# A transformer layer's opening on one core: second-half rows squared sooner, one power for four tiles' norms, high parts of values, keys and queries ahead of low ones

## The chip, the cores and the metric

One core of a Trainium2 chip. Its engines run side by side, each with its own instruction stream: PE (TensorE: matrix products and transposes), DVE (VectorE), ACT (ScalarE), POOL (GpSimd) and SP (SyncE, which here issues nearly all DMAs). The metric is the device time of one execution in microseconds (us); lower is better.

## The reference, cut to what matters

```python
h  = rms_norm(x, norm_mix)                     # x: 1024 tokens x 1024 features, float32
P  = h @ w_in                                  # -> q_A k_A v_A | q_B k_B v_B | gate_A gate_B
A  = neighbourhood_attention(rms_norm(q_A), rms_norm(k_A), v_A, rpb)       # 8 heads of 64 ("na")
Bm = sliding_window_attention(rms_norm(q_B), rms_norm(k_B), v_B, sink, t5) # 8 heads, 2 key heads ("sw")
y  = sigmoid(gate_A) * (A @ w_branch_A) + sigmoid(gate_B) * (Bm @ w_branch_B)
x  = x + y @ w_out
x  = x + (silu(rms_norm(x) @ w_gate) * (rms_norm(x) @ w_up)) @ w_down
```

`rms_norm(z) = z / sqrt(mean(z*z) + 1e-6) * gain`. For queries and keys the mean goes over the 64 elements of a head.

## The kernel before

Every float32 product is made of three matmuls of rounded parts: a high part of an operand (rounded by ACT as it copies) and a low part (what is left, by DVE), high x high, high x low and low x high. Tokens lie in 8 tiles of 128; features in 8 blocks of 128 (index k).

The heads come in six groups (`order`): na heads 0 and 1, then sw heads 0 to 3, and so on. This case is about the opening, which is the projection of group 0 (`projection(0)`) and the first tiles of group 1. PE follows the code's order throughout. In the opening (the `opening` stack) ACT, DVE, POOL and SP do too; after it a scheduler orders these four.

In group 0 the eight token tiles go through two passes, c=0 (tiles 0 to 3) and c=1 (tiles 4 to 7), each tile with a PSUM bank of its own; a pass takes k = 0 to 7, and for each k four chunks, one for a tile. A **chunk** is three matmuls of 384 columns (query, key and value columns of the group) in `multiply`. Group 1 and later go tile by tile, eight chunks each, and PE mixes their chunks with the attention of the heads that are ready.

RMSNorm of x is not applied to x. `row_norm(c)` squares four tiles of x on ACT (`rows`, loaded by `load_rows`), with the sums in `rows_rs` and, after a power of -0.5 on POOL, the tokens' factors there; `rows_eps` is the sum's term that belongs inside the head norms. The gates need the same factors spread along columns: `wide_norm(c, ps)` builds four diagonal matrices on DVE (`diag`), multiplies them by ones on PE, and copies the bank to `wide_rs[c]` on ACT.

`finish(tiles)` takes the finished banks of some tiles: ACT squares queries and keys into `qn`, DVE sums them by head into `ss`, POOL adds `rows_eps` and takes the power -0.5, ACT and DVE write high and low values `v`, and DVE multiplies the bank by the norm into `qn`. Then `layout` gives PE work for later: `keys()` transposes the keys of four tiles into a bank `tk`, `pair()` the queries into `tq`, and ACT writes the high half of each head's key or query times the gain, DVE the low half; SP copies keys to `k2`. `pop(pending)` runs the next of these. The names in the trace: `pj` a chunk's bank, `tk` and `tq`, `wg_kh` and `wg_kl` the high and low weights of block k (`after.split(k)` makes those of group 1 during pass c=1), `wst` and `wg_us` their staging tiles.

Softmax of a head's block: `scores` puts q times k into one of two banks `s`, DVE reads the bank with the bias table `bna` into `E`, ACT takes the exponential. `bias_table` adds the table on DVE just ahead of the first block.

Of the kernel before, what the change touches and what calls it, by code (L numbers as in the profile page):

```python
# [19 lines left out]
HD = 64  # L20
NEG = -1e30
EPS = 1e-6
# [3 lines left out]
def block_kernel(ctx, tc, x, xt, small, w_in, rpb, t5, w_ba, w_bb, w_out, w_gate, w_up, w_down,  # L26
# [76 lines left out]
    mhalf = cst.tile([P, 8], F32, name="mhalf")  # L103
# [7 lines left out]

    def rsqrt_mean(dst, ss, n, width):
        nc.gpsimd.tensor_scalar(dst, ss, 1.0 / n, EPS, op0=ALU.mult, op1=ALU.add)
        nc.gpsimd.tensor_tensor(dst, dst, mhalf[:, :width], ALU.pow)
# [27 lines left out]
    def row_norm(c):  # L142
# [5 lines left out]
        nc.gpsimd.tensor_scalar(rows_eps[:, d], rows_rs[:, d], EPS, 1.0, op0=ALU.mult, op1=ALU.mult)  # L148
        nc.gpsimd.tensor_tensor(rows_rs[:, d], rows_rs[:, d], mhalf[:, 0:4], ALU.pow)

    def wide_norm(c, ps):

        dg = slot_u(f"diag{c}")[:, :512]
# [6 lines left out]
    def load_small():  # L160
        nc.scalar.dma_start(cols, small)
        nc.vector.tensor_scalar_mul(nsink, nsink, -1.0)
        for b in "ab":
            nc.vector.tensor_scalar_mul(gq[b], gq[b], HD ** -0.5)
# [65 lines left out]
    def projection(gi, weights, pending, after=None):  # L230
# [14 lines left out]

        def layout(s0):
            sw = kind == "sw"

            def rev_put(z, own, oth, src, g):
# [9 lines left out]
                nc.scalar.activation(to(z, own), src, AF.Copy, scale=g)  # L259
                nc.vector.scalar_tensor_tensor(to(z, oth), src, g, f(to(z, own)), op0=ALU.mult, op1=ALU.subtract)  # L260
# [12 lines left out]
            def put_both(z, own, oth, src, g):  # L273
                nc.scalar.activation(put(z, own), rows16(src), AF.Copy, scale=g)
                nc.vector.scalar_tensor_tensor(put(z, oth), rows16(src), g, f(put(z, own)),
                                               op0=ALU.mult, op1=ALU.subtract)

            def pair(p_):
                tq = bank("pj", f"tq{gi}_{s0}_{p_}")
                for j in range(4):  # L280
                    nc.tensor.transpose(spot(tq, slice(0, P), j), qns[s0 + j][:, tok(p_)], ident)
                for e in range(2):
                    own, oth = slice(e * HD, e * HD + HD), slice(HD - e * HD, 2 * HD - e * HD)
                    rev_put(q[2 * p_ + e], own, oth, tq[own, :], gq[b][own, :])

            def keys():
# [3 lines left out]
                for e in range(nk):  # L290
                    own, oth = slice(e * HD, e * HD + HD), slice(HD - e * HD, 2 * HD - e * HD)
                    put_both(k1[e], own, oth, tk[own, :], gk[b][own, :])
# [19 lines left out]
        def finish(tiles):  # L312

            norms = {}
            for t, ps in tiles:
                ss = norms[t] = ap.tile([P, 8], F32, tag="ss", name=f"ss{gi}_{t}", bufs=4)
                qn = ap.tile([P, 320], F32, tag="qn", name=f"qn{gi}_{t}", bufs=5)
                nc.scalar.activation(qn[:, :nqk], ps[:, :nqk], AF.Square)
                nc.vector.tensor_reduce(ss[:, :nh], qn[:, :nqk].rearrange("p (h e) -> p h e", e=HD),
                                        axis=AX.X, op=ALU.add)  # L320
                nc.gpsimd.tensor_scalar(ss[:, :nh], ss[:, :nh], 1.0 / HD, rows_eps[:, t:t + 1],
                                        op0=ALU.mult, op1=ALU.add)
                nc.gpsimd.tensor_tensor(ss[:, :nh], ss[:, :nh], mhalf[:, :nh], ALU.pow)  # L323
                qns.append(qn)
            for t, ps in tiles:
                rs = rows_rs[:, t:t + 1]
                if kind == "na":
                    for j in range(nk):
                        src = ps[:, nqk + j * HD:nqk + j * HD + HD]
                        nc.scalar.activation(v[j][:, t, 0, :], src, AF.Copy, scale=rs)  # L330
                        nc.vector.scalar_tensor_tensor(v[j][:, t, 1, :], src, rs, f(v[j][:, t, 0, :]),
                                                       op0=ALU.mult, op1=ALU.subtract)
                else:
# [4 lines left out]
                    if t == 7:  # L338
                        vr = slot_v(f"vr{gi}")[:, :512].rearrange("p (b e) -> p b e", e=HD)
                        nc.sync.dma_start(vr, vnat[idx * T:(idx + 1) * T, :].rearrange("(b p) e -> p b e", p=P))  # L340
                        late_v.append(vr)
                nc.vector.tensor_mul(qns[t][:, :nqk].rearrange("p (h e) -> p h e", e=HD),
                                     ps[:, :nqk].rearrange("p (h e) -> p h e", e=HD),
                                     norms[t][:, :nh].unsqueeze(2).to_broadcast([P, nh, HD]))
# [963 lines left out]
```

## Time and profile before

| | |
|---|---|
| time, median of 3 runs | 1357.77 us (1357.66 to 1359.6) |
| profiled execution | 1355.7 us, of which the span of instructions is 1353.8 |
| PE busy in the span | 97% |
| DVE, ACT, POOL busy | 75%, 50%, 13% |

The span runs from the first to the last instruction; what lies around it (1.9 us) is start and end. PE is the engine to watch: a time in which it waits is a time that the kernel could lose, and there is little of it. Start times in the rows below count from the span's start.

### The profile page before, as it was taken

The numbers are of one execution on the slowest core, as the hardware profiler recorded it, in microseconds if no ns is written. First come the engines' busy times: TensorE is split into PE (matmuls) and PEld (weight loads), VectorE is DVE, ScalarE is ACT, GpSimd is POOL, SyncE is SP. The second block draws the span as 40 slices with busy tenths as digits, with TensorE's granted clock in tenths as the row PEclk, the third lists the DMA queues.
The fourth block names the chain that finished last, engine by engine and source line by source line (L and its number), as shares of the span: only waits on it lengthen the run. The fifth ranks groups of instructions, "written<-read, shape, count | busy, mean of one in ns | idle before, by whom it ended". The sixth has DMA issues, their size and how long they took to land.

```text
span 1353.8 us, 19149 instructions
## 1 busy us (share of the span) xinstructions
PE 1318.6 (97%) x6464; PEld 1134.0 (84%) x6464; DVE 1008.8 (75%) x1989; ACT 675.3 (50%) x1381; POOL 174.6 (13%) x320
## 2 busy tenths in 40 slices
PE   9899999999999999999997999999999999999998
PEld 8799999999887887887886888888888888888887
DVE  5578877887769746878978876766777678798775
ACT  6567866785654324535545433333333346263532
POOL 1345544464220000000000000000000000000000
PEclk9899999999999999999998999999999999999999
DMA  8413223132424335747783433223333246672542
GB/s 284 141 50 83 72 69 96 44 104 67 127 86 164 121 97 179 246 159 223 240 280 103 150 102 99 92 90 117 117 117 109 94 130 236 237 259 71 163 133 86
DMA packets 177571, 184.03 MB, mean 136 GB/s; under 512 B 20496, under 2 KB 125968, under 8 KB 177472
## 3 DMA queue, kind: packets, MB, share of 16 engines
q1 hardware_dynamic: 177216, 182.70, 42.6%
q8 instruction: 51, 0.84, 0.3%
q14 instruction: 48, 0.39, 0.1%
q10 hardware_dynamic: 256, 0.10, 0.0%
HBM read 128.74 MB, written 48.97 MB: 131 GB/s over the span
## 4 chain that ended last, share of the span: by engine, by line
PE 80%; DVE 8%; DMA 6%; ACT 3%; issue 1%; POOL 1%; SPq 1%; DVEq 0%; ACTq 0%; POOLq 0%
PE bankZ L771 5%; PE bankZ L772 5%; PE bankZ L773 5%; PE bankY L773 5%; PE bankY L771 5%; PE bankY L772 5%; PE bankX L773 5%; PE bankX L772 5%; PE bankX L771 5%; PE pj L308 3%; PE pj L309 3%; PE pj L310 3%; PE o L587 3%; PE bankV L772 3%; PE bankV L773 2%; PE bankV L771 2%
## 5 line engine op out<-in xcount | busy, mean ns | idle before, releaser
L537 ACT ACTIVATE E<-E,nm 128x384 f32<-128x384 f32 (+3 forms) x128 | 75.7, 592 | 55.1 <-DVE nm L531 47.3
L539 POOL TENSOR_SCALAR E<-E,nm 128x384 f32<-128x384 f32 (+1 forms) x128 | 76.3, 597 | 118.3 <-DVE nm L538 88.5
L51 DVE TENSOR_TENSOR pl<-tp,ph 128x384 fp32r<-128x384 f32 (+1 forms) x128 | 66.5, 520 | 13.1 <-ACT ph L50 11.6
L50 ACT CAST ph<-tp 128x384 fp32r<-128x384 f32 (+1 forms) x128 | 57.4, 448 | 18.4 <-PE tp L549 17.1
L51 DVE TENSOR_TENSOR f<-f 128x512 fp32r<-128x512 f32 x89 | 58.6, 690 | 10.3 <-ACT f L50 10.2
L50 ACT CAST f<-f 128x512 fp32r<-128x512 f32 x89 | 52.7, 619 | 27.1 <-DMA f<-u_dram 26.6
L549 PE MATMUL tp<-ident,E 128*128 128x128 f32 x352 | 59.7, 273 | 0.0
L323 POOL TENSOR_TENSOR ss<-ss,mhalf 128x4 f32<-128x4 f32 (+1 forms) x48 | 51.8, 1079 | 3.4
L587 PE MATMUL o<-pl,v 128*128 128x256 f32 (+2 forms) x160 | 49.3, 308 | 2.4 <-DVE pl L51 2.3
L549 PEld LDWEIGHTS tp<-ident,E 128*128 128x128 f32 x352 | 45.3, 140 | 5.3 <-POOL E L539 0.4
L587 PE MATMUL o<-ph,v 128*128 128x256 f32 (+2 forms) x160 | 46.3, 303 | 2.4 <-DVE of L570 2.3
L525 PE MATMUL s<-k,q 128*128 128x384 f32 (+1 forms) x128 | 46.6, 364 | 0.0
L1140 POOL TENSOR_TENSOR rs<-rs,mhalf 128x4 f32<-128x4 f32 x2 | 2.1, 1059 | 339.9 <-DVE rs L1139 339.9
L1154 ACT ACTIVATE sg<-sg 128x512 f32<-128x512 f32 x44 | 27.9, 633 | 35.4 <-DVE sg L1153 35.2
L526 PE MATMUL s<-k,q 128*128 128x384 f32 (+1 forms) x128 | 41.5, 324 | 0.0
L531 DVE CUSTOM_DVE_ANT_0 E<-s,bsw,cols 128x384 f32<-128x384 f32 (+1 forms) x64 | 37.0, 578 | 5.3 <-PE s L526 4.1
L773 PE MATMUL bankV<-f,f_5l 128*128 128x512 f32 x88 | 35.1, 399 | 3.8 <-DVE f_5l L51 3.8
L531 DVE CUSTOM_DVE_ANT_0 E<-s,bna 128x384 f32<-128x384 f32 (+1 forms) x64 | 33.2, 519 | 6.4 <-PE s L526 5.9
L538 DVE RECIPROCAL nm<-nm 128x1 f32<-128x1 f32 x128 | 20.4, 160 | 23.0 <-ACT E L537 21.6
L773 PE MATMUL bankY<-f,f_6l 128*128 128x512 f32 x88 | 35.1, 399 | 2.2 <-DVE f_6l L51 2.2
L771 PE MATMUL bankV<-f,f_5h 128*128 128x512 f32 x88 | 34.9, 397 | 2.4 <-ACT f_5h L50 2.4
L51 DVE TENSOR_TENSOR f_2l<-wg_s,f_2h 128x512 fp32r<-128x512 f32 x22 | 15.1, 691 | 27.6 <-ACT f_2h L50 27.6
(799 smaller groups left out, 4556.7 us busy)
## 6 DMA issues: line engine op xcount, KB each, us to landing
f<-u_dram SPq DMA_DIRECT2D x77, 256.0 KB
wg_s<-in_w_gate_dram SPq DMA_DIRECT2D x22, 512.0 KB
u_dram<-uT SPq DMA_DIRECT2D x33, 256.0 KB
sg<-g_dram SPq DMA_DIRECT2D x32, 256.0 KB
g_dram<-go SPq DMA_DIRECT2D x24, 256.0 KB
u_dram<-tau SPq DMA_DIRECT2D x22, 256.0 KB
u_dram<-tbu SPq DMA_DIRECT2D x22, 256.0 KB
f<-f_dram SPq DMA_DIRECT2D x18, 256.0 KB
```

The lines of the kernel that those rows point to most:

```text
L50: a = nc.scalar.copy(hi, src)
L51: b = (eng or nc.vector).tensor_tensor(lo, src, f(hi), ALU.subtract)
L323: nc.gpsimd.tensor_tensor(ss[:, :nh], ss[:, :nh], mhalf[:, :nh], ALU.pow)
L525: nc.tensor.matmul(s[:, :n], qs, k1[hd["kl"]][:, ks], start=True, stop=False)
L531: nc.vector.tensor_tensor_reduce(E[:, :n], s[:, :n], hd["bias"](qb), -1.0, sk if sw else 1e30, ALU.add, ALU.min, nm[:, 0:1])
L537: nc.scalar.activation(E[:, :m], E[:, :m], AF.Exp, bias=nm[:, 0:1], scale=-1.0, accum_out=nm[:, 1:2])
L539: nc.gpsimd.tensor_scalar(E[:, :n], E[:, :n], nm[:, 1:2], 1.0, op0=ALU.mult, op1=ALU.mult)
L549: nc.tensor.transpose(tp[:, tok(j)], hd["E"][qq][:, ko:ko + P], ident)
L587: nc.tensor.matmul(hd["O"][half][:, (a - half * 4) * P:(z + 1 - half * 4) * P], v[:, kb].rearrange("p a e -> p (a e)"), pp[:, (a - q0) * P ...
L771: nc.tensor.matmul(ps, hi[:, tok(j)], bh, start=first, stop=False, skip_group_check=True)
L772: nc.tensor.matmul(ps, hi[:, tok(j)], bl, start=False, stop=False, skip_group_check=True)
L773: nc.tensor.matmul(ps, lo[:, tok(j)], bh, start=False, stop=end, skip_group_check=True)
```

## The change

Seven edits, all but one in the opening.

1. The rows of tiles 4 to 7 are loaded behind the second piece of group 1's weights, not after all features of x; the third and fourth pieces and the tables follow them on SP.
2. `row_norm(1)` is issued after block k=4 of pass c=1, not after the pass: ACT has the squares between the high keys and the high queries of the first half.
3. `finish` of four tiles makes one sum and one power of 16 columns on POOL, not four of each with 4 columns. The division by 64 is gone: it sits in `HD * EPS` and in a key gain of 8 rather than a query gain of 1/8.
4. In `finish` all high values, then all low values, then the products with the norm; before, each tile had its own high, low, high, low, product. This holds for later na groups too, two heads at a time.
5. For group 0 both high key parts go ahead of both low ones, and the same for queries (`both`).
6. Transposes of the first half's keys and queries are popped at k=4 and 5 of pass c=1, not 6 and 7. Group 1's weight blocks 0 to 2 are split at k=4, block 3 at k=6, and 4 to 7 at the end. The second half's queries use a bank `t`.
7. `wide_norm` moves from tiles 2 and 3 of group 1 to the first gate's projection, and its diagonals lie in a slot of the weight pool. `qn` has 7 buffers, not 5.

```diff
+        dg = wp.tile([P, 512], F32, tag="whi", name=f"diag{c}", bufs=NWU)
...
+        def both(parts):
+            if gi:
+                for part in parts:
+                    part()()
+            else:
+                for low in [part() for part in parts]:
+                    low()
...
-                ss = norms[t] = ap.tile([P, 8], F32, tag="ss", name=f"ss{gi}_{t}", bufs=4)
...
-                nc.gpsimd.tensor_scalar(ss[:, :nh], ss[:, :nh], 1.0 / HD, rows_eps[:, t:t + 1],
-                                        op0=ALU.mult, op1=ALU.add)
-                nc.gpsimd.tensor_tensor(ss[:, :nh], ss[:, :nh], mhalf[:, :nh], ALU.pow)
...
+            if n == 1:
+                nc.gpsimd.tensor_scalar(ss, ss, 1.0, rows_eps[:, t0:t0 + 1], op0=ALU.mult, op1=ALU.add)
+            else:
+                nc.gpsimd.tensor_tensor(norms, norms, rows_eps[:, t0:t0 + n].unsqueeze(2).to_broadcast([P, n, nh]),
+                                        ALU.add)
+            nc.gpsimd.tensor_tensor(ss, ss, mhalf[:, :n * nh], ALU.pow)
...
+            for t, ps in tiles if kind == "na" else ():
+                for j in range(nk):
+                    nc.vector.scalar_tensor_tensor(v[j][:, t, 1, :], ps[:, nqk + j * HD:nqk + j * HD + HD],
...
-                    if c and k >= 4:
-                        after.split(k - 4)
-                    if c and k >= 6:
+                    for u in {4: (0, 1, 2), 6: (3,)}.get(k, ()) if c else ():
+                        after.split(u)
+                    if c and k in (4, 5):
                         pop(pending)
+                    if c and k == 4:
+                        row_norm(1)
...
-            row_norm(1)
...
-                if gi == 1 and t in (2, 3) and k == 7:
-                    wide_norm(t - 2, bank("pj", f"wide{t}"))
...
+                if i == 0 and not half and k in (1, 4):
+                    wide_norm(k // 4, bank("pj", f"wide{k}"))
...
-        for u in range(4):
+        for u in range(2):
+            weights[1].load(u)
+        for t in range(4, 8):
+            load_rows(t)
+        for u in range(2, 4):
             weights[1].load(u)
...
-        for t in range(4, 8):
-            load_rows(t)
```

ACT's order around the first half's keys and queries (`k_0`, `k_1`, `q_0`, `q_1` are the two heads' operands; `rows_286` and its like are tiles 4 to 7 of x). Before:

```order
L274 ACTIVATE k_0_302<-tk_0_561,cols 64x512
L274 ACTIVATE k_1_303<-tk_0_561,cols 64x512
L50 CAST wg_3h<-wg_1s 128x384
L259 ACTIVATE q_0_298<-tq_0_0_590,cols 64x512
L259 ACTIVATE q_1_299<-tq_0_0_590,cols 64x512
L50 CAST wg_4h<-wst_130 128x384
L50 CAST wg_5h<-wst_130 128x384
L50 CAST wg_6h<-wst_131 128x384
L50 CAST wg_7h<-wst_131 128x384
L146 ACTIVATE rows_286,rows_rs<-rows_286 128x1024
```

Of the change, the same place on ACT:

```order
L282 ACTIVATE k_0_302<-tk_0_528,cols 64x512
L282 ACTIVATE k_1_303<-tk_0_528,cols 64x512
L142 ACTIVATE rows_256,rows_rs<-rows_256 128x1024
L142 ACTIVATE rows_258,rows_rs<-rows_258 128x1024
L142 ACTIVATE rows_260,rows_rs<-rows_260 128x1024
L142 ACTIVATE rows_262,rows_rs<-rows_262 128x1024
L267 ACTIVATE q_0_298<-tq_0_0_560,cols 64x512
L267 ACTIVATE q_1_299<-tq_0_0_560,cols 64x512
L50 CAST wg_3h<-wg_1s 128x384
L50 CAST wg_4h<-wst_130 128x384
```

The four squares of x have moved from behind the weight blocks to a place ahead of the queries, and block 3 of the weights from ahead of the queries to behind them.

POOL's order for the second half (`ss_4` to `ss_7` are head sums of tiles 4 to 7). Before:

```order
L149 TENSOR_TENSOR rows_rs<-rows_rs,mhalf 128x4
L321 TENSOR_SCALAR ss_4_622<-ss_4_622,rows_eps 128x4
L323 TENSOR_TENSOR ss_4_622<-ss_4_622,mhalf 128x4
L321 TENSOR_SCALAR ss_5_628<-ss_5_628,rows_eps 128x4
L323 TENSOR_TENSOR ss_5_628<-ss_5_628,mhalf 128x4
L321 TENSOR_SCALAR ss_6_634<-ss_6_634,rows_eps 128x4
L323 TENSOR_TENSOR ss_6_634<-ss_6_634,mhalf 128x4
L321 TENSOR_SCALAR ss_7_640<-ss_7_640,rows_eps 128x4
L323 TENSOR_TENSOR ss_7_640<-ss_7_640,mhalf 128x4
```

Of the change, POOL from the first half's power on:

```order
L335 TENSOR_TENSOR ss_0_457<-ss_0_457,mhalf 128x16
L143 TENSOR_SCALAR rows_rs<-rows_rs 128x4
L144 TENSOR_SCALAR rows_eps<-rows_rs 128x4
L145 TENSOR_TENSOR rows_rs<-rows_rs,mhalf 128x4
L333 TENSOR_TENSOR ss_4_613<-ss_4_613,rows_eps 128x16
L335 TENSOR_TENSOR ss_4_613<-ss_4_613,mhalf 128x16
L331 TENSOR_SCALAR ss_0_680<-ss_0_680,rows_eps 128x5
```

Eight instructions of 4 columns have become two of 16.

DVE's order ahead of the first softmax (`E_0_0` is the first block's scores out of their bank; `ss_1` to `ss_3` belong to tiles of group 1). Before:

```order
L342 TENSOR_TENSOR qn_1_734<-pj_1_708,ss_1_733 128x320
L275 SCALAR_TENSOR_TENSOR k_0_302<-tk_4_750,cols,k_0_302 64x512
L319 TENSOR_REDUCE ss_2_813<-qn_2_814 128x5
L275 SCALAR_TENSOR_TENSOR k_1_303<-tk_4_750,cols,k_1_303 64x512
L260 SCALAR_TENSOR_TENSOR q_0_298<-tq_4_0_772,cols,q_0_298 64x512
L342 TENSOR_TENSOR qn_2_814<-pj_2_743,ss_2_813 128x320
L260 SCALAR_TENSOR_TENSOR q_1_299<-tq_4_0_772,cols,q_1_299 64x512
L503 TENSOR_TENSOR bna_294<-brna_295,bna_294 128x384 x2
L531 ISA E_0_0_787,nm_0_0_788<-s_0_0_784,bna_294 128x256
```

Of the change:

```order
L327 TENSOR_REDUCE ss_2_784<-qn_2_785 128x5
L356 TENSOR_TENSOR qn_1_716<-pj_1_690,ss_1_715 128x320
L283 SCALAR_TENSOR_TENSOR k_0_302<-tk_4_732,cols,k_0_302 64x512
L283 SCALAR_TENSOR_TENSOR k_1_303<-tk_4_732,cols,k_1_303 64x512
L268 SCALAR_TENSOR_TENSOR q_0_298<-tq_4_0_754,cols,q_0_298 64x512
L268 SCALAR_TENSOR_TENSOR q_1_299<-tq_4_0_754,cols,q_1_299 64x512
L518 TENSOR_TENSOR bna_294<-brna_295,bna_294 128x384 x2
L356 TENSOR_TENSOR qn_2_785<-pj_2_725,ss_2_784 128x320
L327 TENSOR_REDUCE ss_3_832<-qn_3_833 128x5
L546 ISA E_0_0_769,nm_0_0_770<-s_0_0_766,bna_294 128x256
```

The sum `ss_2` now stands ahead of the low keys and queries of the second half, and the sum `ss_3` ahead of the first softmax block.

## Rows read from the trace of the kernel before

**Rows 1.** Windows: span, busy time of PE, PEld, DVE, ACT, POOL; granted clock, DMA.

```profile
60.00:70.00 10.00, 7.50 (x33) 6.93 (x33) 4.62 (x9) 3.79 (x9) 4.12 (x7) 0.73 0.15 33
80.00:345.00 265.00, 261.76 (x1683) 252.98 (x1682) 216.29 (x630) 192.35 (x508) 136.35 (x254) 1.00 0.26 72
```

**Rows 2.** Timeline of PE, pass c=1 ending, group 1 begun: start, length, instruction.

```profile
43.05 0.60 PE L281 MATMUL tq<-ident,qn 128*128 128x128 f32 x4
43.41 0.42 PE L308 MATMUL pj<-wg_0h,h 128*128 128x384 f32 x1
...
45.43 0.34 PE L310 MATMUL pj<-wg_3h,h 128*128 128x384 f32 x1
46.81 0.44 PE L308 MATMUL pj<-wg_4h,h 128*128 128x384 f32 x1 [1.04 <-ACT wg_4h L50]
...
48.11 0.34 PE L308 MATMUL pj<-wg_5h,h 128*128 128x384 f32 x1
```

**Rows 3.** Waits of PE from 42 to 80: sum, times, longest.

```profile
PE tk L289 <- DVE qn L342: 4.6, 4, 1.2
```

**Rows 4.** Timeline of PE around the second half's keys.

```profile
54.36 0.33 PE L308 MATMUL pj<-wg_1h,h 128*128 128x384 f32 x1
...
60.75 0.67 PE L308 MATMUL pj<-wg_2h,h 128*128 128x384 f32 x1
...
65.79 0.33 PE L308 MATMUL pj<-wg_6h,h 128*128 128x384 f32 x1
```

**Rows 5.** Timeline of PE around the two wide norms.

```profile
66.66 0.34 PE L310 MATMUL pj<-wg_7h,h 128*128 128x384 f32 x1
...
70.06 0.44 PE L308 MATMUL pj<-wg_0h,h 128*128 128x384 f32 x1 [1.51 <-ACT wide_rs L158]
...
74.68 1.05 PE L157 MATMUL wide<-diag,ones 128*128 128x128 f32 x8
75.49 0.42 PE L308 MATMUL pj<-wg_0h,h 128*128 128x384 f32 x1
...
76.63 0.34 PE L525 MATMUL s<-k,q 128*128 128x384 f32 x1
```

**Rows 6.** Timeline of ACT, the same stretch.

```profile
45.54 0.68 ACT L259 ACTIVATE q<-tq,cols 64x512 fp32r<-64x512 f32 x1 [0.94 <-DVE q L260]
...
47.90 1.06 ACT L146 ACTIVATE rows<-rows 128x1024 f32<-128x1024 f32 x1
...
52.20 1.21 ACT L318 ACTIVATE qn<-pj 128x256 f32<-128x256 f32 x4
```

**Rows 7.** Timeline of DVE, the same stretch.

```profile
46.25 0.76 DVE L260 SCALAR_TENSOR_TENSOR q<-tq,cols,q 64x512 fp32r<-64x512 f32 x1 [0.75 <-ACT q L259]
47.04 0.56 DVE L51 TENSOR_TENSOR wg_4l<-wst,wg_4h 128x384 fp32r<-128x384 f32 x1
...
52.62 1.40 DVE L319 TENSOR_REDUCE ss<-qn 128x4 f32<-128x256 f32 x4 [2.66 <-ACT qn L318]
...
58.62 0.42 DVE L342 TENSOR_TENSOR qn<-pj,ss 128x256 f32<-128x256 f32 x1 [0.17 <-POOL ss L323]
...
70.43 0.49 DVE L342 TENSOR_TENSOR qn<-pj,ss 128x320 f32<-128x320 f32 x1
...
71.94 1.03 DVE L503 TENSOR_TENSOR bna<-brna,bna 128x384 f32<-128x384 f32 x2
73.00 0.42 DVE L531 CUSTOM_DVE_ANT_0 E<-s,bna 128x256 f32<-128x256 f32 x1
```

**Rows 8.** Timeline of POOL: the first half's first norm.

```profile
30.31 0.27 POOL L321 TENSOR_SCALAR ss<-ss,rows_eps 128x4 f32<-128x4 f32 x1
```

**Rows 9.** Groups by form on POOL: count, busy us, mean ns of one, idle before.

```profile
L323 POOL TENSOR_TENSOR ss<-ss,mhalf 128x4 f32<-128x4 f32 x32 | 32.6, 1020 | 2.3
L323 POOL TENSOR_TENSOR ss<-ss,mhalf 128x5 f32<-128x5 f32 x16 | 19.1, 1196 | 1.2
```

**Rows 10.** Timeline of SP: issues of group 1's later weight pieces.

```profile
25.97 4.01 SPq L202 DMA_DIRECT2D wst<-in_w_in_dram  x6
```

More of the change, by code (lines that the diff above doesn't have):

```diff
@@ L244, in projection @@
         qns, late_v = [], []
+        SIDES = [(slice(e * HD, e * HD + HD), slice(HD - e * HD, 2 * HD - e * HD)) for e in range(2)]
+        def both(parts):
[5 more added lines that the diff above has]
+                    low()
         def layout(s0):
@@ L274, in put_both @@
                 nc.scalar.activation(put(z, own), rows16(src), AF.Copy, scale=g)
-                nc.vector.scalar_tensor_tensor(put(z, oth), rows16(src), g, f(put(z, own)),
-                                               op0=ALU.mult, op1=ALU.subtract)
+                return lambda: nc.vector.scalar_tensor_tensor(put(z, oth), rows16(src), g, f(put(z, own)),
+                                                              op0=ALU.mult, op1=ALU.subtract)
             def pair(p_):
-                tq = bank("pj", f"tq{gi}_{s0}_{p_}")
+                tq = bank("pj" if gi or not s0 else "t", f"tq{gi}_{s0}_{p_}")
                 for j in range(4):
                     nc.tensor.transpose(spot(tq, slice(0, P), j), qns[s0 + j][:, tok(p_)], ident)
-                for e in range(2):
-                    own, oth = slice(e * HD, e * HD + HD), slice(HD - e * HD, 2 * HD - e * HD)
-                    rev_put(q[2 * p_ + e], own, oth, tq[own, :], gq[b][own, :])
+                both([lambda e=e, own=own, oth=oth: rev_put(q[2 * p_ + e], own, oth, tq[own, :], gq[b][own, :])
+                      for e, (own, oth) in enumerate(SIDES)])
             def keys():
@@ L289, in keys @@
                     nc.tensor.transpose(spot(tk, slice(0, nk * HD), j), qns[s0 + j][:, nq * HD:nqk], ident)
-                for e in range(nk):
-                    own, oth = slice(e * HD, e * HD + HD), slice(HD - e * HD, 2 * HD - e * HD)
-                    put_both(k1[e], own, oth, tk[own, :], gk[b][own, :])
+                both([lambda e=e, own=own, oth=oth: put_both(k1[e], own, oth, tk[own, :], gk[b][own, :])
+                      for e, (own, oth) in enumerate(SIDES[:nk])])
+                for e, (own, oth) in enumerate(SIDES[:nk]):
                     for c in ([slice(0, T)] if s0 and kind == "sw" else
```

35 lines of the change are left out of this document (17 added, 18 removed).

## The prediction

> **What bounds the kernel now.** Start with the windows [rows 1]: from 80 to 345 us, the attention, PE is busy 261.76 of 265.00. PE sets the end there, and whatever another engine saves is free time. Then take the window 60 to 70 of the opening: PE is busy 7.50 of 10.00, and the granted clock is 0.73, between the two levels (1.2 and 2.4 GHz), so that a part of it ran at the lower one. So the change can bring only what PE loses in the opening. To read that, take the timeline of PE and ask of each start when it would have come had nothing held PE. The yardstick is a chunk (three matmuls): from 70.06 to 74.68 [rows 5] run eight chunks and two score matmuls of 384 columns, 26 matmuls in 4.62; with about 0.1 of it for the first start after a wait that is 0.173 a matmul, 0.52 a chunk. Four losses stand out.
>
> - **T1, weights of group 1.** The last matmul of block 3 starts at 45.43. One matmul and one chunk later, block 5 is due at 46.12; it starts at 48.11 [rows 2], 1.99 late. What is waited for is block 4's high part. ACT made it late: at 45.54 it had stood idle 0.94, waiting for the low query of the first head, before it could write the second [rows 6].
> - **T2, second half's keys.** Block 1 of tile 2 starts at 54.36, so `tk` is due at 54.88. Four transposes cost 0.36 (43.05 to 43.41 [rows 2]), so block 2 is due at 55.24; it starts at 60.75 [rows 4]: 5.5 late. The view of waits puts it down to the four products `qn`, 4.6 us in four [rows 3], and each of those waits for POOL's `ss` [rows 7].
> - **T3, half clock.** From 60.75 to 65.79 [rows 4] is 5.04. In it lie four chunks (2.08), four transposes (0.36) and two score matmuls of 256 columns (0.23), 2.67 at full clock: 2.37 lost, in the window with the clock of 0.73, directly behind the long wait of T2.
> - **T4, first wide norm.** Its last chunk's last matmul starts at 66.66, the wide norm is due at 66.83, and its eight matmuls cost 0.81 (74.68 to 75.49, the second one, which waited for nothing). So the next chunk is due at 67.64; it starts at 70.06 [rows 5]: 2.42 late, most of it the wait for the copy by ACT.
>
> Together 1.99 + 5.5 + 2.37 + 2.42 = 12.3.
>
> **The change part by part.** Up to 43.41 PE does the same work; the transposes only move inside pass c=1. From 43.41 back, 12 chunks (6.24) and two transposes of four (0.72): `tk` of the first half now comes at about 36.4.
>
> *First half's norms.* POOL starts them at 30.31 and its add took 0.27 [rows 8]. The add is now a 16-column one with a broadcast operand, which no row shows: between 0.27 (flat) and 1.02 (the price of a small two-operand instruction here); I take 0.3, since it has no power in it. The power of 16 columns is not shown either. Rows 9 give 1.020 for 4 columns and 1.196 for 5: 0.16 to 0.18 a column. Bounds: 1.02 if a column costs nothing, 4.08 if four tiles cost four times one. By the slope of 0.16, 1.02 + 12 x 0.16 = 2.9, my value: it is nearest to the only two rows that differ in columns. Then POOL is done at 30.31 + 0.3 + 2.9 = 33.5, and four products of 0.42, which overlap to about 0.37 each [rows 7], end at 35.1. `tk` at 36.4 finds them, with 1.3 to spare.
>
> The Trainium skill (GPSIMD Engine Reference, section 3.1 Elementwise — side-by-side cycle accounting) gives GpSimd about 2.6 cycles an element at 1.2 GHz for an elementwise instruction. By it 12 more columns of a lane would cost 26 ns (an estimate), the power would stay near 1.05, and the saving would come to 10.3 rather than 9.9; the slope in rows 9 speaks against it for a power.
>
> *First half's keys and queries, T1.* ACT has the high keys at about 37.0 to 38.4 (0.68 each [rows 6]), then the four squares of x, 1.06 each [rows 6], to 42.6, then the two high queries: 43.9. The waits of ACT for DVE (0.94 of it seen) are gone. DVE follows with two low queries of 0.76 [rows 7], 45.4, and with `wg_3l`, 0.56 less some overlap: 45.9. PE wants `wg_3l` for the second matmul of block 3 in tile 0, at 43.41 + 3 x 0.52 + 0.173 = 45.14. So a new wait of **0.8** stands in T1's place, bounds 0 and 2.0 (that of before). Behind it blocks 4 to 7 follow at ACT's pace: four took 46.22 to 47.90, 0.42 each [rows 6], less than a chunk.
>
> *Loads.* The rows go ahead of two weight pieces and the tables on SP. Before, the pieces' issues began at 25.97 and ended by 29.98 [rows 10]; ACT first reads them at about 44.3 after the change. Four issues of 512 KB put them back by some 6 us, which 14 us cover; if the cover were gone it would cost what exceeds it. The squares want rows at 38.4; before they were read at 47.90.
>
> *Second half's norms, T2.* The squares of x no longer stand between the weights and `qn`: ACT is through with block 7 at 45.95, and with the four squares of `qn` (1.21 [rows 6]) at 47.2. DVE, behind its low weights (47.7), has the four sums (1.40 [rows 7]) at 49.2; POOL adds and takes the power, 3.2, to 52.5 with a hand-over; the low values hide in that; four products end at 54.0. PE comes to `tk` at 43.41 + 18 x 0.52 + 0.8 = 53.6: a wait of **0.4**, bounds 0 (a flat power) and 1.6 (a power of 4.08). T2's 5.5 go, and with them the long idle ahead of T3, so I put T3's 2.37 as won: the wait of 1.51 ahead of 70.06 was followed by 26 matmuls at full speed [rows 5]. If the clock falls all the same, 2.37 of the saving is gone.
>
> *Wide norms, T4.* At the gate their 2 x 0.81 of PE stay; the diagonals and factors are 280 us old, so PE should wait for none; the copy could hold the next user of the bank. Bounds 0 and 2.42; I take 0.
>
> *What is late next.* PE now runs into the first softmax earlier, while DVE's list ahead of `E_0_0` is as long. Scores have two banks, so the third block, `s_0_2`, waits for `E_0_0`. Before, `E_0_0` began at 73.00 and `s_0_2` at 76.63 [rows 5, 7]: 3.6 apart, no wait. After, tile 2 of group 1 is complete on PE at about 58.1 (54.0 + 0.36, six chunks 3.12, transposes 0.36, scores 0.23). From there the chain is a square on ACT (0.44, an estimate from rows 6, 1.21 for four of 256 columns and more columns here), sum and product of 0.49 each [rows 7], four low keys and queries (2.96, by 0.74 of [rows 7]), the bias table 1.03, product and sum 0.98 again, and `E_0_0` 0.42: 6.8. PE's own work to `s_0_2` is ten chunks and a score, 5.56. The difference is a new wait of **1.2**; bounds 0 (the sums fill gaps) and 2.4 (twice it). `E_0_0` of the changed order stands behind `ss_3`, which it did not before.
>
> Edits of gains and eps, buffers of `qn` and the bank of `tq` add no instruction. The order of values in later na groups changes DVE and ACT only, under the 261.76 of 265 of [rows 1].
>
> **The sum.** 12.3 - (0.8 + 0.4 + 1.2) = 9.9 us saved. The profiled execution took 1355.7, which would become 1345.8. The median of the runs is 1357.77, 2.1 above that execution; I carry the saving over: 1357.8 - 9.9 = **1347.9**. With all four terms at their dear ends (2.0, 1.6, 2.4 and T4 kept) the saving is 12.3 - 8.4 = 3.9; with none of them, 12.3. A measurement of this kernel tells a change from none at about 0.2%, 2.7 us.
>
> **The rivals.**
>
> *A, the forecast*: saved 7.5 to 11.5, chance 0.62.
>
> *B, half given back*: the new waits are at their dear ends. A power at 4.08 takes 1.6 at the second `tk`, T1 keeps 2.0, `s_0_2` waits 2.4, and the wide norm at the gate keeps 1.2, half of T4: 12.3 - 7.2 = 5.1, 1352.7. For it: three of the four prices are not seen in a row, and ACT's list ahead of `wg_4h` is longer by four squares of x. Against it: each needs its own bad end. Saved 3 to 7.5: chance 0.21.
>
> *C, given back in the attention*: DVE has 216.29 busy of the 265 from 80 to 345 [rows 1], and an earlier PE could find it behind, block by block. Then the time stays near 1357. Against it: PE's idle there is 3.2 us in all, so DVE has kept up, and it starts no later than before. Chance 0.09.
>
> *D, slower through the power*: if POOL takes P for 16 columns, the second `tk` loses P - 2.9 more, and the first, with 1.3 to spare, P - 4.2. Saving 9.9 is used up at (P - 2.9) + (P - 4.2) = 9.9, P = 8.5, or 0.53 a column, and from about 9.9 on the time is over 0.2% slower than before; at P = 11 it is 1357.8 + 5.0 = 1362.8. For it: all of a power's rows are short ones. Against it: 4 columns cost 1.02 in all, 0.26 each at most [rows 9]. Chance 0.04.
>
> *E, all of it*: a power whose columns cost next to nothing and no new wait: 12.3, 1345.5. Against it: the fifth column of rows 9. Chance 0.04. (That power is the one that the Trainium skill's GPSIMD Engine Reference, section 3.1, would give.)
>
> **How the numbers follow.** The likeliest is A, 1347.9. The range reaches down to 1344.5, which holds E and a point of scatter between runs, and up to 1352.8, which holds B's point; beyond it lie C, D and the upper tail of B, under 2 in 10. Faster by over 0.2%: A, B and E, 0.87. Within 0.2%: C, with little of D, 0.09. Slower: D, 0.04.
>
> **What would show it.** In the trace after: POOL's 128x16 power near 2.9; first `tk` at 36.4 without a wait; PE's wait for `wg_3l` of 0.8 near 45; the wait at the second `tk` under 1 us; the granted clock of 50 to 70 at 1.00; a chunk, not a wide norm, at 60; a wait of `s_0_2` for `E_0_0` near 1.2; the wide norms near 345 with no wait behind them. I am wrong if the power is far over 4, if the rows land late (ACT waiting for a DMA at 38), or if the clock falls all the same behind a shorter wait.

## The result and the profile after

The changed kernel took 1348.78 us, median of 6 runs (1347.57 to 1350.6), against 1357.72 for the kernel before in the same session (6 runs): ratio 0.9936, 95% interval 0.9923 to 0.9949, or 8.7 us less by that ratio. The forecast was 1347.9 and 9.9. A second session with the same kernel (`e12` below) gave 0.9951 (0.9933 to 0.9969), 6.6 less. The first saving lies in the band of rival A (7.5 to 11.5), the second in that of B (3 to 7.5), so the time alone does not tell the two apart; the trace does, since the new waits are not at B's dear ends. The profiled execution took 1350.09, with a span of 1348.3.

The windows show the opening first. The columns are those of [rows 1], which had 7.50 busy and a clock of 0.73 in the second stretch:

```profile
50.00:60.00 10.00, 10.00 (x63) 9.93 (x62) 4.77 (x16) 4.14 (x8) 5.94 (x7) 1.00 0.16 39
60.00:70.00 10.00, 8.70 (x51) 8.32 (x51) 7.65 (x21) 3.57 (x11) 4.16 (x7) 1.00 0.29 67
80.00:345.00 265.00, 260.03 (x1668) 251.14 (x1667) 212.95 (x627) 188.67 (x503) 134.86 (x251) 1.00 0.28 76
```

PE now works without a gap where the second half's keys held it, and the clock is full. One hole of 1.3 is left in the second window. The view of PE's waits from 25 to 80 names everything that is left; it had 4.6 for `tk` alone [rows 3]:

```profile
PE s L540 <- DVE nm L546: 1.3, 1, 1.3
PE pj L316 <- DVE wg_3l L51: 0.9, 1, 0.9
```

These are the two new waits that the sum had put at 1.2 and 0.8. The timeline of PE has their places, and those of the four losses of before:

```profile
36.34 0.60 PE L296 MATMUL tk<-ident,qn 128*128 128x128 f32 x4
...
46.26 0.45 PE L316 MATMUL pj<-wg_3l,h 128*128 128x384 f32 x1 [0.85 <-DVE wg_3l L51]
...
54.01 0.60 PE L296 MATMUL tk<-ident,qn 128*128 128x128 f32 x4
54.37 0.42 PE L315 MATMUL pj<-wg_2h,h 128*128 128x384 f32 x1
...
65.29 0.45 PE L540 MATMUL s<-k,q 128*128 128x384 f32 x1 [1.30 <-DVE nm L546]
```

The second half's keys are transposed in 0.36 with no wait, and block 2 behind them starts at 54.37; before it started at 60.75 [rows 4]. The third score block starts at 65.29, before at 76.63 [rows 5]: 11.34 sooner, of which 1.62 are the two wide norms that have only moved. So 9.7 is won by then. The same start is the yardstick of the experiments. The first loads shift everything behind them by up to 1.2 between the executions shown here, so it is counted from the first matmul of pass c=1, 25.83 here and 25.86 before (25.16 to 26.38 in all runs): the **opening stretch** is 39.46 here and 50.77 before. In a second execution of the changed kernel it was 39.45, while whole times of one kernel scatter by up to 5.7 us. The other engines do not always shift as far as PE does (in `e3`, PE by 0.67 and `wg_3l` by 0.28), so a difference of up to 0.4 in the stretch can be the loads'.

POOL shows the disputed price:

```profile
29.80 0.21 POOL L333 TENSOR_TENSOR ss<-ss,rows_eps 128x16 f32<-128x16 f32 x1
30.09 2.92 POOL L335 TENSOR_TENSOR ss<-ss,mhalf 128x16 f32<-128x16 f32 x1
...
49.77 2.91 POOL L335 TENSOR_TENSOR ss<-ss,mhalf 128x16 f32<-128x16 f32 x1
```

The power of 16 columns takes 2.92; the sum with the broadcast operand takes 0.21, less than the 0.27 that was its lower bound.

At the gate the wide norms wait for nothing and hold nobody (PE's timeline; the next instruction starts 0.89 and 0.81 behind each):

```profile
337.05 1.05 PE L153 MATMUL wide<-diag,ones 128*128 128x128 f32 x8
337.94 0.38 PE L564 MATMUL tp<-ident,E 128*128 128x128 f32 x2
...
340.59 1.05 PE L153 MATMUL wide<-diag,ones 128*128 128x128 f32 x8
341.40 0.47 PE L417 MATMUL pg<-h,wg_1h 128*128 128x512 f32 x1
```

What the forecast did not have stands in the attention, at the projection of the third group:

```profile
102.22 0.41 PE L315 MATMUL pj<-wg_0h,h 128*128 128x384 f32 x1 [0.56 <-DVE qn L356]
...
104.55 0.63 PE L289 MATMUL tq<-ident,qn 128*128 128x128 f32 x4 [0.72 <-DVE q L268]
```

Before, the first of these starts ran on without a wait and the second had waited 0.29. Matching PE's instructions one by one, the lead of 11.34 is 10.02 behind the second of them: 1.3 is given back by then, 1.2 of it at these two starts. `e8` below shows which edit does it. PE ends the attention's last product at 396.80, before at 404.61. That is 7.8 sooner (of the 11.34, the two moved wide norms take 1.6, the third group 1.3, and smaller pieces on the way 0.6), which lies between the 8.7 and 6.6 of the two sessions.

The spans differ by only 5.5, since the profiled execution after lost about 2.3 more in the windows behind the attention; the section on the hardware returns to it.

### The profile page after: what moved, and what is told of

It is laid out like the page before. It is cut to its first block, busy times and chain, and to the rows that moved or that the text cites. A ratio compares the mean times of both kernels' runs of the same rounds, so it can differ in the third digit from the quotient of the medians.

```text
span 1348.3 us, 19145 instructions
## 1 busy us (share of the span) xinstructions
PE 1316.1 (98%) x6464; PEld 1132.6 (84%) x6464; DVE 1005.4 (75%) x1989; ACT 673.4 (50%) x1381; POOL 170.6 (13%) x308
## 4 chain that ended last, share of the span: by engine, by line
PE 84%; DVE 7%; DMA 4%; ACT 3%; issue 2%; SPq 1%; POOL 0%; ACTq 0%; DVEq 0%; POOLq 0%
PE bankZ L788 6%; PE bankZ L790 6%; PE bankZ L789 6%; PE bankY L790 5%; PE bankY L788 5%; PE bankY L789 5%; PE bankX L789 5%; PE bankX L790 5%; PE bankX L788 5%; PE pj L317 4%; PE pj L316 4%; PE pj L315 4%; PE bankV L789 3%; PE o L602 3%; PE bankV L790 3%; PE bankV L788 3%
## 5 line engine op out<-in xcount | busy, mean ns | idle before, releaser
L335 POOL TENSOR_TENSOR ss<-ss,mhalf 128x4 f32<-128x4 f32 (+2 forms) x42 | 49.4, 1176 | 3.1
```

## The experiments

All times are compared through the kernel before of the same session, whose median moved from 1357.1 (first four) to 1356.09 (next four) and 1355.62 (last four). A difference of under 0.15% between two changed kernels is within their intervals; there the opening stretch decides.

| kernel | third score block | opening stretch | median, us | ratio to before (interval) |
|---|---|---|---|---|
| before | 76.63 | 50.77 | 1357.72 | |
| changed | 65.29 | 39.46 | 1348.78 | 0.9936 (0.9923 to 0.9949) |
| e1 four powers | 66.46 | 40.38 | 1349.4 | 0.9946 (0.9931 to 0.9961) |
| e2 squares late | 65.20 | 39.35 | 1349.02 | 0.9942 (0.9928 to 0.9957) |
| e3 wide norms back | 66.56 | 39.78 | 1348.02 | 0.9939 (0.9922 to 0.9955) |
| e4 values by tile | 69.23 | 43.40 | 1352.8 | 0.9971 (0.9959 to 0.9983) |
| e5 low behind high | 67.14 | 40.76 | 1349.22 | 0.994 (0.9923 to 0.9957) |
| e6 blocks and bias sooner | 63.19 | 37.42 | 1344.83 | 0.9916 (0.9901 to 0.9931) |
| e7 one power alone | 76.96 | 50.65 | 1357.26 | 1.0004 (0.9995 to 1.0013) |
| e8 high values alone | 76.54 | 50.75 | 1356.44 | 1.0003 (0.9994 to 1.0012) |
| e9 one power and high values | 73.51 | 48.03 | 1354.91 | 0.9995 (0.9985 to 1.0004) |
| e10 wide norms moved alone | 73.74 | 49.26 | 1355.93 | 1.0001 (0.999 to 1.0012) |
| e11 squares late, wide norms back | 68.18 | 40.59 | 1349.89 | 0.9958 (0.9943 to 0.9973) |
| e12 changed, again | 65.48 | 39.45 | 1348.8 | 0.9951 (0.9933 to 0.9969) |

In `e3` and `e11` the wide norms' 1.62 of PE work lie inside the stretch and are taken off; in `e10` they have left it, against `before`, and are added.

**e1, four powers** in the changed kernel (the edit is shortened):

```diff
-            nc.gpsimd.tensor_tensor(norms, norms, rows_eps[...].to_broadcast([P, n, nh]), ALU.add)
-            nc.gpsimd.tensor_tensor(ss, ss, mhalf[:, :n * nh], ALU.pow)
+                nc.gpsimd.tensor_scalar(ss[:, :nh], ss[:, :nh], 1.0, rows_eps[:, t:t + 1], op0=ALU.mult, op1=ALU.add)
+                nc.gpsimd.tensor_tensor(ss[:, :nh], ss[:, :nh], mhalf[:, :nh], ALU.pow)   # for each of the tiles
```

> The changed kernel with four sums and four powers of 4 columns in place of one of 16 (the one power undone, everything else kept). Read: the start of the first matmul of the third score block, 65.29 in the changed kernel, and PE's wait at the second half's key transposes, none there. My theory (the 5.5 us came from several edits, and any of them alone can be missed): with the sums ready from about 48.4 POOL takes 4 x 1.47 and ends near 54.3, the last product near 54.8, PE is due at 54.0 to 54.3: a wait of about 0.5, so 65.8 and a time 0.5 longer. Rival (the one power is what pays, 5.9 us of POOL against 3.2): a wait of 2.7, and 68.

The stretch is 0.92 longer. A wait of 0.5 for `qn` was named rightly but in the wrong place: it stands at the first half's keys, and only some 0.2 is at the second half's (0.57 from the first transpose to the chunk behind, rather than 0.36). The expectation had no term for the first keys. The rival's 68 is out. One power is worth about a microsecond here, not POOL's 2.7.

**e2, squares late** in the changed kernel:

```diff
-                    if c and k == 4:
-                        row_norm(1)
...
+            row_norm(1)
             pending += finish([(t, done[t]) for t in range(4, 8)])
```

> The changed kernel with the squares of x for tiles 4 to 7 behind the weight blocks again, as before, but the rows' loads early. My theory: the wait for the low block 3 (0.85) goes, since the queries come 4.2 earlier on ACT; the squares then end near 48.3, the norms' power starts near 50.0 rather than 49.8, and the products end near 54.7, while PE comes to the keys at 53.2: a wait of 1.5. Net the third score block at 65.9, time +0.6. Rival (the squares' place is what made the second half late; moved back they cost their 4.2): third score block at 68.5 or later and half a clock stretch.

PE's timeline at the second half's keys and at the third score block:

```profile
54.15 1.29 PE L296 MATMUL tk<-ident,qn 128*128 128x128 f32 x4 [1.09 <-DVE qn L356]
55.20 0.42 PE L315 MATMUL pj<-wg_2h,h 128*128 128x384 f32 x1
...
65.20 0.45 PE L539 MATMUL s<-k,q 128*128 128x384 f32 x1 [0.40 <-DVE nm L545]
```

The wait for the low block 3 is gone. At the second keys PE waits 1.09, and the four transposes, one behind each product, take 1.05 rather than 0.36: 1.8 in all, where 1.5 was expected. The net was to be +0.6 and is -0.1: the later PE is, the less it waits for the first softmax (0.4 rather than 1.3), which the expectation had left out. The rival falls. With the rest of the change in place, squares sooner are worth nothing: what they cost at block 3 and at the softmax they give back at the keys.

**e3, wide norms back** in the changed kernel: `wide_norm` again behind chunk 7 of tiles 2 and 3 of group 1, the diagonals in their old slots.

```diff
-                if i == 0 and not half and k in (1, 4):
-                    wide_norm(k // 4, bank("pj", f"wide{k}"))
...
+                if gi == 1 and t in (2, 3) and k == 7:
+                    wide_norm(t - 2, bank("pj", f"wide{t}"))
```

> The changed kernel with the two wide norms back in group 1's projection. My theory: T4's 2.42 was a follow-on of the late keys (ACT was behind with keys and queries when the copy was due), so now only short waits stand there, about 0.75 and 0.4 for banks, and the wait of the third score block (1.3) goes since DVE gains that time. Third score block near 66.6, against 65.29 + 1.62 of PE work at the gate = 66.9: time within 0.5 of the changed kernel, rather 0.3 less. Rival (the place of the wide norm is what cost 2.42): time 1.1 to 2.4 longer.

Third score block 66.56 (66.6 expected), a stretch 0.3 longer without the moved work, and no time lost; the 0.3 may be the loads' (block 3 waits 1.23 here, not 0.85). PE waits 0.65 for `wide_rs`, where before it waited 1.51 and lost 2.42 in all. So the place of the wide norms alone is not what cost T4, and the rival falls.

That T4 followed from the late keys of T2 is not shown. In `e9` below these keys come 2.1 sooner than before, and the wait for `wide_rs` is 1.73; in `e7` they come 1.3 later, and it is 0.68 (PE reaches the wide norm 1.3 later there, when ACT is through with these parts). What the wait goes with is ACT's list ahead of the copy. Before, then in `e9`, a high query stands directly ahead of it, and the copy starts 0.88 and 1.11 behind the end of the wide norm's matmuls:

```profile
68.86 0.68 ACT L259 ACTIVATE q<-tq,cols 64x512 fp32r<-64x512 f32 x1
69.44 0.57 ACT L158 COPY wide_rs<-wide 128x512 f32<-128x512 f32 x1
```

```profile
65.73 0.68 ACT L259 ACTIVATE q<-tq,cols 64x512 fp32r<-64x512 f32 x1
66.32 0.57 ACT L158 COPY wide_rs<-wide 128x512 f32<-128x512 f32 x1
```

In `e3` the high keys and queries are done at 58.11, before the wide norm begins, and the copy starts 0.04 behind the end of its matmuls:

```profile
56.73 1.38 ACT L267 ACTIVATE q<-tq,cols 64x512 fp32r<-64x512 f32 x2 [0.61 <-PE tq L289]
...
59.42 0.59 ACT L154 COPY wide_rs<-wide 128x512 f32<-128x512 f32 x1
```

`e3` has edit 5, which lets ACT write both high keys and both high queries without a low one between; the kernel before, `e7` and `e9` have not. That edit 5 is what ended T4 is likely and was not tried: it would take `e3` with edit 5 undone.

**e4, values by tile** in the changed kernel (the products with the norm back in the same loop too):

```diff
                     for j in range(nk):
+                        src = ps[:, nqk + j * HD:nqk + j * HD + HD]
                         nc.scalar.activation(v[j][:, t, 0, :], src, AF.Copy, scale=rs)
+                        nc.vector.scalar_tensor_tensor(v[j][:, t, 1, :], src, rs, f(v[j][:, t, 0, :]), ...)
```

> The changed kernel with the values in the old order (high, low, high, low, product, tile by tile) in all na groups. My theory: the products of tiles 1 to 3 now follow the one power at the pace of the values, about 1.3 to 1.46 a tile, since ACT waits for DVE's low value and DVE for ACT's high one: the first half's products end near 37.4 and the first key transposes, due at 36.3, wait 1.1; the second half's wait is 2 to 3. Third score block 3 to 4 us later, near 68.8, time +3 to +4. Rival (values are hidden under the power, their order earns nothing): 65.3 to 65.8 and no change of time.

A stretch 3.94 longer, as expected (+3 to +4), and a ratio of 0.9971, which makes it 2.7 us longer than `e12` and 4.7 longer than the first session of the changed kernel. By PE's starts the first half's keys take 1.3 of the 3.94, the second half's 2.5, and the clock behind them 1.4; the wait for the first softmax gives 1.3 back. DVE's timeline shows the mechanism, the one power having ended shortly before 54.01:

```profile
54.01 0.42 DVE L353 TENSOR_TENSOR qn<-pj,ss 128x256 f32<-128x256 f32 x1 [2.33 <-POOL ss L335]
54.35 0.28 DVE L342 SCALAR_TENSOR_TENSOR v<-pj,rows_rs,v 128x64 fp32r<-128x64 f32 x1
55.01 0.28 DVE L342 SCALAR_TENSOR_TENSOR v<-pj,rows_rs,v 128x64 fp32r<-128x64 f32 x1 [0.38 <-ACT v L341]
55.21 0.41 DVE L353 TENSOR_TENSOR qn<-pj,ss 128x256 f32<-128x256 f32 x1
```

From product to product 1.20: the values of the next tile lie between, and the low one waits 0.38 for its high one from ACT.

**e5, low behind high** in the changed kernel, for keys and queries:

```diff
-            if gi:
+            if True:
                 for part in parts:
                     part()()
```

> The changed kernel with each head's low key or query right behind its high part again (edit 5 undone; values stay high first). My theory: ACT waits for DVE 0.75 between two heads' keys and again between their queries, so the low block 3 comes 0.75 later (wait 1.6 rather than 0.85), and the second half's four low parts end some 1.3 later ahead of the first softmax: third score block at 67.3 (65.29 in the changed kernel), time +2. Rival (ACT's waits are covered): 65.3 to 65.6, same time.

The stretch is 1.30 longer (2.0 expected; the third score block at 67.14 is near the expected 67.3 only because the first loads were 0.55 later here). Block 3 is late by 1.4 in two waits, the third score block waits 1.8. The whole time, 0.994 of before, does not show it; the difference is inside the intervals, so of the time this run tells nothing.

**e7 and e8, one power alone and high values alone**, each in the kernel before: the edits 3 and 4 of the change.

> The kernel before with one power for four tiles alone. My theory: without the new order of values the products follow the power at the values' pace of 1.3 to 1.46 a tile, so the second half's products end near 61.7 rather than 60.5: the chunk behind the keys starts near 61.9 (60.75 before), and the time is 1 longer than before. Rival (POOL's 5.9 against 3.2 is what held the keys): that chunk at 58.0, time 2.7 less or more, as the clock then does not fall.

> The kernel before with the new order of values alone (all high, all low, then the products). My theory: POOL's four powers still end near 60.05, one every 1.47, and the last product behind them, so nothing is won: the chunk behind the keys starts at 60.5 to 60.8 (60.75 before), time within 0.5 of before. Rival (the order of values alone is worth the 4 us that its undoing cost in the changed kernel): that chunk near 57, time 4 less.

Neither moved the time: 1.0004 and 1.0003. The block behind the keys starts at 62.08 in `e7`, of which 0.45 is a later first load (61.9 expected; 60.75 before), and at 60.66 in `e8`. In `e8` DVE's products come one every 1.46, each released by its power:

```profile
57.07 0.42 DVE L345 TENSOR_TENSOR qn<-pj,ss 128x256 f32<-128x256 f32 x1 [0.39 <-POOL ss L323]
58.53 0.42 DVE L345 TENSOR_TENSOR qn<-pj,ss 128x256 f32<-128x256 f32 x1 [1.03 <-POOL ss L323]
59.98 0.42 DVE L345 TENSOR_TENSOR qn<-pj,ss 128x256 f32<-128x256 f32 x1 [1.03 <-POOL ss L323]
```

In `e7` the power of 2.98 ends in one go, and then the products follow at 57.84, 59.04, 60.23 and 61.42, at the 1.19 of the values, with no wait for POOL behind the first:

```profile
57.84 0.43 DVE L346 TENSOR_TENSOR qn<-pj,ss 128x256 f32<-128x256 f32 x1 [1.62 <-POOL ss L328]
...
59.04 0.41 DVE L346 TENSOR_TENSOR qn<-pj,ss 128x256 f32<-128x256 f32 x1
```

There were two chains of nearly the same length side by side, POOL's and that of ACT with DVE; to cut one shows the other.

`e8` shows one thing more. Its opening is that of before, so PE is not ahead, and still it has the two waits at the third group that the changed kernel has. PE's timeline in `e8`:

```profile
113.31 0.41 PE L308 MATMUL pj<-wg_0h,h 128*128 128x384 f32 x1 [0.53 <-DVE qn L345]
...
115.63 0.63 PE L281 MATMUL tq<-ident,qn 128*128 128x128 f32 x4 [0.70 <-DVE q L260]
```

The same starts before:

```profile
112.74 0.33 PE L308 MATMUL pj<-wg_0h,h 128*128 128x384 f32 x1
...
114.57 0.63 PE L281 MATMUL tq<-ident,qn 128*128 128x128 f32 x4 [0.29 <-DVE q L260]
```

And in `e4`, where PE is 6.8 ahead of the kernel before but the values have their old order:

```profile
105.95 0.33 PE L315 MATMUL pj<-wg_0h,h 128*128 128x384 f32 x1
...
107.76 0.63 PE L289 MATMUL tq<-ident,qn 128*128 128x128 f32 x4 [0.28 <-DVE q L268]
```

Between the last chunk ahead of the first start and the second start, the ten traces with the new order of values lose 0.8 to 1.3 against the kernel before (`e8` 1.2); `e4`, `e7` and `e10`, which keep the old one, lose 0.0, 0.0 and 0.2. So it is edit 4 in the later na groups that gives this back, not PE's being early. The product that the first start waits for stands at 111.69 on DVE before and at 112.75 in `e8`:

```profile
111.69 0.41 DVE L342 TENSOR_TENSOR qn<-pj,ss 128x256 f32<-128x256 f32 x1
```

```profile
112.75 0.41 DVE L345 TENSOR_TENSOR qn<-pj,ss 128x256 f32<-128x256 f32 x1
```

Of that tile's two low values, one is written at 108.73 before; in `e8` both come behind the low query, at 112.36. PE ends the attention 1.3 later in `e8` than before (405.93).

**e9, one power and high values** in the kernel before: both at once.

> The kernel before with one power and the new order of values together (each alone moved the time by nothing). My theory: now neither chain of 1.2 to 1.46 a tile is left, so the four products follow the power in one go: power 54.3 to 57.2, products to 58.9, the chunk behind the keys at 59.1 rather than 60.75, third score block at 75.0 rather than 76.63, time 1.6 less than before. Rival (the two add up to the nothing that they gave alone): 60.7, 76.6 and no change.

The block behind the keys starts at 58.64 (59.1 expected), behind a single wait:

```profile
57.59 1.29 PE L289 MATMUL tk<-ident,qn 128*128 128x128 f32 x4 [2.94 <-DVE qn L349]
58.64 0.42 PE L308 MATMUL pj<-wg_2h,h 128*128 128x384 f32 x1
```

So together they pay where each alone paid nothing. A wait of 2.94 is left at these keys, which the changed kernel has not. The opening stretch is 2.74 shorter, 1.1 more than expected, since part of the loss of clock is gone (0.88 over 56 to 70 rather than 0.76). The time, though, was expected 1.6 shorter and is 0.7 (not told from none by its interval): PE ends the attention only 1.3 sooner. At the third group it has the two waits that come with edit 4 (0.6 and 0.7; before, 0.3 in all); they give back 1.2.

**e10, wide norms moved alone**, in the kernel before.

> The kernel before with the wide norms moved to the gate alone. My theory: at its old place the first one cost 0.81 of work and 2.42 of wait, but behind it the third score block then runs into the first softmax (73.0 and later), so it starts near 74.0 rather than 76.63; 1.6 of that is work that the gate takes over: time 1.0 less than before. Rival (all of T4 is won): third score block at 72.6, time 2.4 less.

Third score block 73.74 (74.0 expected); the stretch without the moved work is 1.5 shorter (1.0 expected, 2.4 by the rival), with a new wait of 0.6 for the first softmax. The time did not change (1.0001), so even that is not seen at the end. PE ends the attention 0.5 sooner; the third group takes 0.2.

**e11, squares late and wide norms back**, in the changed kernel: `e2` and `e3` together.

> The changed kernel with two parts undone that cost nothing when undone alone: the squares of x late and the wide norms back in group 1. My theory: what is left (one power, values high first, keys and queries high first, transposes sooner) carries the whole gain: third score block at 67.4, against 66.9 for equal, time within 0.7 of the changed kernel. Rival (each covers for the other, so both undone cost T4's 2.4 or more): third score block at 69 or later, time 2 to 3 longer.

Third score block 68.18, a stretch 1.13 longer than the changed kernel's: 0.6 more than expected. PE waits at the second half's keys, where the four transposes also take 1.05 rather than 0.36, and once for a bank that the product of a tile of group 1 holds up:

```profile
54.31 1.29 PE L296 MATMUL tk<-ident,qn 128*128 128x128 f32 x4 [1.16 <-DVE qn L356]
55.36 0.42 PE L315 MATMUL pj<-wg_2h,h 128*128 128x384 f32 x1
...
67.03 0.44 PE L315 MATMUL pj<-wg_0h,h 128*128 128x384 f32 x1 [1.00 <-DVE qn L356]
```

The time is 1.1 above that of `e12` in the same session, inside the intervals. Two parts that each can go at little loss (-0.1 and 0.3) cost 1.1 together: they cover for each other in part, and neither theory had the right size.

**e6, blocks and bias sooner**: the changed kernel with the two new waits taken away (the line that added the table later goes; the comment is not in the code).

```diff
-                    for u in {4: (0, 1, 2), 6: (3,)}.get(k, ()) if c else ():
+                    for u in {4: (0, 1, 2, 3), 5: (4,)}.get(k, ()) if c else ():
...
-            for k in range(4, 8):
+            for k in range(5, 8):
                 after.split(k)
...
+            if gi == 0 and t0 == 4:
+                heads[0]["bias"] = bias_table(heads[0])      # between the low values and the products
```

> A version meant to beat the changed kernel: weight block 3 is split with blocks 0 to 2, where ACT and DVE stand idle, block 4 ahead of the first half's queries, and the bias table is added while POOL takes the second half's power. My theory: both new waits of the changed kernel (0.85 for the low block 3, 1.30 for the third score block) go, no other comes: third score block near 63.3, time 2.0 less than the changed kernel's 1348.8. Rival (the waits only move: to a later weight block, to the second keys, or into the attention): third score block at 64.5 or later, or the time stays at 1348 to 1349.

Third score block 63.19 (63.3 expected), a stretch 2.04 shorter, 0.2 of wait left in it (for `wg_5l`), and 1344.83, the fastest of all: 0.9916 (0.9901 to 0.9931), 11.4 less than before by that ratio. Its interval lies below that of `e12` and overlaps with that of the first session; the stretch is clear. The two waits at the third group stay (0.4 and 0.7). DVE adds the bias table while POOL takes the power, and the first softmax comes at 56.40 rather than 64.82:

```profile
50.38 1.02 DVE L520 TENSOR_TENSOR bna<-brna,bna 128x384 f32<-128x384 f32 x2
52.11 1.42 DVE L358 TENSOR_TENSOR qn<-pj,ss 128x256 f32<-128x256 f32 x4 [0.72 <-POOL ss L335]
...
56.40 0.42 DVE L548 CUSTOM_DVE_ANT_0 E<-s,bna 128x256 f32<-128x256 f32 x1
```

**e12, the changed kernel again.**

> The changed kernel once more, for what differs between executions. Theory: the opening repeats (third score block at 65.2 to 65.4), while the profiled execution of the changed kernel lost 1.7 in a half-clock stretch at 520.8 that not every execution has; so the span differs by 1 to 3 although the opening is the same. Rival: the stretch at 520 belongs to the change and comes back.

The opening repeats to 0.01, with all of PE's starts 0.2 later from the first loads on. The loss of clock behind the attention came back, some 8 us later, so the rival is not ruled out by this run.

## Why the prediction was right

*The four losses.* All four went. T1's 1.99 became a wait of 0.85 for `wg_3l` (0.8 forecast). T2 was forecast to keep 0.4 and keeps none, which is luck: the products end at 54.13 (54.0 forecast), but PE comes to the keys only at 54.01, not at 53.6. T3: the granted clock is 1.00 from 50 to 70, and the long wait is gone. T4's place is empty.

*The new wait.* The third score block waits 1.30 for the first softmax (1.2 forecast), by the list on DVE that the prediction walked through.

*What T2 hung on.* The prediction read the products as waiting for POOL alone and gave the order of values no price. `e7` and `e8` show a second chain of the same step beside POOL's, so the one power by itself would have won nothing; the time came out right since edits 3 and 4 were made together. It also counted the squares' place among what frees T2; in `e2` putting them back costs 1.8 at the keys, which two other waits give back.

*The power.* 2.92 against 2.9 from the slope of two rows. By the 2.6 cycles an element of the Trainium skill (GPSIMD Engine Reference, section 3.1) it would have been about 1.05 (an estimate); the trace disagrees, for this operation.

*The loads.* The rows come in time: ACT squares them at 38.40 with no wait for a DMA, and the blocks behind them on SP are not late.

*What was mis-sized.* In the opening 9.7 was won where 9.9 was forecast. The step that failed is the sentence that the order of values in later na groups changes DVE and ACT only, under the 261.76 of 265: it was put at nothing, and it makes PE wait at two starts of the third group, which cost 1.2 (`e8` has them with PE not ahead, `e4` with the old order has them not). Rival C had a loss in the attention, but by another road, an earlier PE that finds DVE behind; `e4`, 6.8 ahead, loses nothing at these starts. Another 0.6 of the lead goes between there and the end of the attention. `e7` and `e10`, which keep the old order, lose about 0.8 from the third score block to that end, and what takes it was not tried. The half clock behind the attention, which both traces of the changed kernel have and that of the kernel before has not, is a further 1.8 that the forecast had no term for; whether it belongs to the change stays open (last section).

*What each edit is worth* was not separated in the prediction, and the runs show that it can't be added up. Undone alone in the changed kernel, the values' order costs 3.9 in the opening stretch, keys and queries high first 1.3, the one power 0.9, the wide norms' place 0.3 and the squares' nothing. Done alone in the kernel before, the power and the values' order each bring nothing, and together 2.7 (`e9`). Edit 6 and the early loads of edit 1 were neither undone nor done alone. `e11`, which has them with edits 3, 4 and 5, is 8.6 shorter than before, the wide norms' work taken off; so most of the gain needs something that `e11` has and `e9` has not, and of that only edit 5 has a price. T2 was two chains of equal length at one spot (`e7`, `e8`, `e9`). That T3 followed from T2 rests on the clock's rows alone: in `e9`, with one wait in place of four, part of it went.

## What to carry to other kernels

Where an engine waits in equal steps (here four times 1.2, a step of 1.46), look for every chain that has this step, not only for the one that the wait names: as long as two run side by side, shortening one shows nothing. Then price what comes next by walking the other engine's list up to its next consumer; here that gave both new waits to 0.1, and moving two small pieces of work into idle time removed them. Undo parts of a change one at a time and also do them alone: a part that can go without loss may still cover for another. And ask of an edit what it does outside the place that it is for: the order of values paid in the opening and cost 1.2 in a later group (a version with the new order in the opening alone was not run).

## What the runs showed of the hardware

The clock fell by different amounts behind waits of different kinds. Over 56 to 70 us, behind PE's waits for the second half's keys, the granted clock was 1.00 in `e2` (one wait of 1.09); 0.88 in `e4` (three waits, 2.0 in all) and in `e9` (one of 2.94); 0.76 before and in `e8` (four, 4.6 and 4.5 in all), and 0.63 in `e7` (one of 2.9 and three more, 5.1 in all). What decides it was not tried further.

A stretch behind the attention in which the granted clock falls to 0.50, the lower of the two levels (522 to 524 in the changed kernel), is in some traces and not in others. Windows from 515 to 535, first the changed kernel, then `e12`, then `e6`:

```profile
515.00:535.00 20.00, 16.92 (x66) 13.16 (x66) 12.95 (x21) 11.20 (x18) 0.00 (x0) 0.91 0.65 199
```

```profile
515.00:535.00 20.00, 16.04 (x63) 12.40 (x62) 12.66 (x20) 11.43 (x19) 0.00 (x0) 0.91 0.65 216
```

```profile
515.00:535.00 20.00, 16.85 (x73) 13.26 (x73) 15.95 (x26) 10.45 (x18) 0.00 (x0) 1.00 0.81 274
```

At 0.91 over 20 us it costs about 1.8 of full clock. `e1` and `e5` show it there too, the kernel before and the other experiments do not. A stretch of the same size (0.91 over the 20 us) stands between 420 and 440 in `e1`, `e5`, `e8` and `e9`, the last two made from the kernel before: such a loss does not need the whole change. Each kernel but the changed one has a single trace, so the traces do not tell whether its place hangs on the execution or on the kernel. It is large enough to hide what one edit of an opening brings, which is why the experiments are read in the opening stretch.
